# Stick breaking in a hybrid decoder trunk: the softplus rows of later key tiles summed on GpSimd for one product with the matrix of ones

## The chip, the cores and the metric

The kernel runs on one core of a Trainium2 chip. The metric is device time in microseconds of one execution; the time of a kernel is the median of its runs. Beside these runs there is one execution with the hardware profiler on, whose trace is quoted here. The core has five instruction queues that run in order and meet through semaphores: TensorE (PE, with its weight loads as PEld), VectorE (DVE), ScalarE (ACT), GpSimd (POOL) and SyncE (SP), which issues the transfers.

## The reference

Two layers of a decoder trunk on 512 tokens of width 1024, fp32. A layer normalizes its input, projects it once, and feeds five mixers: sparse attention with an index, forgetting attention, stick-breaking attention, native sparse attention and cross-attention into 256 memory tokens. Gated outputs are merged and projected back. The change is in the third mixer, which has four heads of 64:

```
z = einsum('bqhd,bshd->bhqs', q_blk, k) * scale
strict = (s_pos[None, :] < t[:, None])
log_keep = where(strict, log_sigmoid(-z), 0.0)
later = cumsum(log_keep, axis=3, reverse=True) - log_keep
a = where(strict, exp(log_sigmoid(z) + later), 0.0)
out = einsum('bhqs,bshd->bqhd', a, v)
```

For a key s, `later` is the sum of log_keep over all keys behind s and before the query. Since log_sigmoid(-z) is minus the softplus of z, and log_sigmoid(z) is z minus the softplus, the exponent is z minus the sum of the softplus over s itself and all later keys.

## The kernel before

All products that matter to precision are made of parts: an fp32 operand is split into a high part, rounded to the type fp32r that TensorE takes, and a low part, the rest; `wload` does this for every weight tile (whi on ScalarE, wlo on VectorE, line 269 and 270), and a projection (`proj`) is 24 products of 128x512.

Stick breaking is `sb_attn(pr)`, run for two pairs of heads in each layer, so for eight heads in all. Scores stand with keys in the partitions: key tile j (0 to 3, 128 keys) against the queries from 128 j on, so tile 0 is 512 columns wide, tile 1 384, tile 2 256, tile 3 128 (kept as 256, the front half zero). `begin` (line 941) makes the scores z of a tile in PSUM and then, on ScalarE and VectorE, its softplus t (`sp_t`, three buffers under the tag P). `store` (972) splits t into a high and a low row, SP[j] (the tile `sp`). `middle` (961) subtracts, by products with constant matrices added onto z, the softplus of all later keys: within the tile with a triangular matrix of -1 (`ntri`), and for each later tile with a matrix of -1 everywhere (`nones`), a product each for the high and the low row; then ScalarE takes the exponential. At the end of a pair the four tiles and two heads are multiplied with v (Yc).

Tiles are taken in the order 3, 2, 1, 0, and the `middle` of a tile stands behind the `begin` of the next. This is woven by `weave` with other work: the memory projection beside the first pair of heads, the query and index projections beside the second. A list scheduler of the framework then orders each engine's queue by its own estimates, so the places of the woven work are not fixed by the code. Its queues are in order on the chip: an instruction that waits holds up all behind it.

The pool `st` holds NST = 28 slots of 128x512 fp32 for whatever a step needs (q and k rows, squares, rotary terms); GpSimd's only work is to fill halves of K tiles with zeros (`k_stack`, line 476).

Of the kernel before, what the change touches and what calls it, by code (L numbers as in the profile page):

```python
# [10 lines left out]
F32 = mybir.dt.float32  # L11
F32R = mybir.dt.float32r
# [9 lines left out]
T = 512  # L22
KT = 8
# [2 lines left out]
EPS = 1e-6  # L26
NEG = -1e30
REPL = -3e38
NST = 28

IN_LAYOUT = (
    ('dsa_q', 256), ('dsa_ckv', 128), ('idx_q', 128), ('idx_k', 32), ('idx_w', 4), ('dsa_z', 256),
# [154 lines left out]
def trunk(ctx: ExitStack, tc: tile.TileContext, xt, memt, pos, wall, small, vec, ca, cb, out):  # L187
    nc = tc.nc
    dep_info = mybir.DependencyInfo(mybir.DependencyClass.NoSync, mybir.DependencyReason.DATA)

    def after(ins, *earlier):
        for e in earlier:
            if e is not None:
                tc.add_manual_dep(ins.ins, e.ins.name, dep_info, reason="issue order")

    def pool(name, bufs=1, **kw):
        return ctx.enter_context(tc.tile_pool(name=name, bufs=bufs, **kw))

    const = pool("const")
    big = pool("big")  # L200
    wts = pool("wts")
    st = pool("st", bufs=NST)
    wk = pool("wk")
# [4 lines left out]
    def slot(name, dt=F32, shape=(128, 512)):  # L208
        return st.tile(list(shape), dt, name=name, tag="st")

    def bank(name, tag, shape=(128, 512)):
        return ps.tile(list(shape), F32, name=name, tag=tag, bufs={"pj": 3, "S": 2, "T": 3}[tag])
# [33 lines left out]
    ntri = const.tile([128, 128], F32R, name="ntri")  # L246
    nones = const.tile([128, 128], F32R, name="nones")
# [10 lines left out]
    def mm(out_, lhsT, rhs, start, stop, **kw):  # L258
        return nc.tensor.matmul(out_, lhsT, rhs, start=start, stop=stop, **kw)  # L259
# [6 lines left out]
    def split(raw, hi, lo, scale=None):  # L266

        if scale is None:
            nc.scalar.activation(hi, raw, AF.Copy)  # L269
            nc.vector.tensor_sub(lo, raw, hi.bitcast(F32))  # L270
        else:
            nc.scalar.activation(hi, raw, AF.Copy, scale=scale)
            nc.vector.scalar_tensor_tensor(lo, raw, scale, hi.bitcast(F32), op0=OP.mult, op1=OP.subtract)
# [113 lines left out]
    def lnexp(*a, **k):  # L387
        i = nc.scalar.activation(*a, **k)
        after(i, state["set"])
        state["ln"].append(i)  # L390
        return i
# [57 lines left out]
    f32 = lambda ap: ap.bitcast(F32)  # L449
# [179 lines left out]
    def y_tiles():  # L629
        a = wk.tile([128, 2, T], F32R, name="yhi", tag="yhi", bufs=2)  # L630
        b = wk.tile([128, 2, T], F32R, name="ylo", tag="ylo", bufs=2)
        return a, b
# [52 lines left out]
    def layer(l, xs, begin):  # L685
        vo = l * V_L
        lv = SimpleNamespace(begin=begin)
# [242 lines left out]
        def sb_attn(pr):  # L930
            SPW = [512, 384, 256, 256]
            if pr == 0:
                sp = big.tile([128, 6, T], F32R, name="sp", tag="xa")
                lv.SP = [[sp[:, 2 * min(j, 2) + s, 256 * (j == 3):256 * (j == 3) + SPW[j]] for s in range(2)] for j in range(4)]
                for s in range(2):
                    nc.vector.memset(f32(lv.SP[3][s][:, 0:128]), 0.0)
            SP = lv.SP
            out = {}

            held = wk.tile([128, 1280], F32, name="sb_a", tag="sb_a", bufs=1)  # L940
            first_a = [held[:, 0:512], held[:, 512:896], held[:, 896:1152], held[:, 1152:1280]]

            def begin(e, j):

                h = 2 * pr + e
                n, w = SPW[j], T - 128 * j
                ks = slice(128 * j, 128 * j + 128)
                z = bank("sbz", "S" if j % 2 else "T")[:, :n]
                mm(z, lv.KC[h][:, ks], lv.QC[h][:, T - n:], True, False)
                mm(z, lv.KlC[h][:, ks], lv.QC[h][:, T - n:], False, False)  # L950
                mw = n - w + 128
                mm(z[:, :mw], identb, sbm[:, 256 - mw:], False, True)
                zw = z[:, n - w:]
                t = wk.tile([128, T], F32, name="sp_t", tag="P", bufs=3)[:, :w]
                nc.scalar.activation(t, zw, AF.Abs)
                lnexp(t, t, AF.Exp, scale=-1.0)
                lnexp(t, t, AF.Ln, bias=ones1)
                nc.vector.scalar_tensor_tensor(t, zw, 0.0, t, op0=OP.max, op1=OP.add)
                return e, j, z, t

            def middle(e, j, z, t):

                n = SPW[j]
                for jj in range(3, j - 1, -1):
                    for s in range(2):
                        mm(z[:, n - SPW[jj]:], ntri if jj == j else nones, SP[jj][s], False, jj == j and s == 1, skip_group_check=True)
                w = T - 128 * j
                a = first_a[j] if e == 0 else wk.tile([128, T], F32, name="sb_a", tag="PT", bufs=5)[:, :w]
                lnexp(a, z[:, n - w:], AF.Exp)
                out[e, j] = a  # L970

            def store(e, j, z, t):
                shi, slo = (x[:, SPW[j] - (T - 128 * j):] for x in SP[j])
                nc.vector.tensor_copy(shi, t)
                nc.vector.tensor_sub(slo, t, f32(shi))

            one = None
            for e in range(2):
                for j in (3, 2, 1, 0):
                    new = begin(e, j)  # L980
                    if one:
                        middle(*one)
                    store(*new)
                    one = new
                    yield
            middle(*one)

            Y = bank("Yc", "T")
            last = None
            for j in (0, 1, 2, 3):  # L990
                for e in (1, 0):
                    h = 2 * pr + e
                    m = mm(Y[64 * e:64 * e + 64, 128 * j:], lv.VC[:, j, 64 * h:64 * h + 64], out[e, j], j == 0, j == 3, skip_group_check=True)
                    after(m, last)
                    last = m
            if pr == 0:
                lv.YC = y_tiles()
            y = slot("yC")
            nc.vector.tensor_mul(y, Y, lv.ZC[0][:, pr])
            split(y, lv.YC[0][:, pr], lv.YC[1][:, pr])  # L1000
# [376 lines left out]
        if l == 0:  # L1377
            run(chain(memory_rows(), take(sp1, 1)))
            cast_constants()
            prio[0] = 3000  # L1380
            ln_phase()
            weave((sb_attn(0), 8), (chain(silu2('sb_z', lv.ZC), take(ixp, 1), take(sp1, 1), take(ixp, 1), mp), 10))
        else:
            run(take(sp1, 1))
            ln_phase()
            weave((sb_attn(0), 8), (chain(silu2('sb_z', lv.ZC), take(ixp, 1), take(sp1, 1), take(ixp, 1), mp), 10))
        tk = topk()
        nsa = nsa_proj()
        weave((sb_attn(1), 8), (chain(memq_proj(), ixp, silu2('mem_z', lv.ZE), take(nsa, 2)), 12))
        tanh_phase()  # L1390
        lv.acc = big.tile([128, KT, T], F32, name="acc", tag="xa")
# [41 lines left out]
```

## Time and profile before

| | us |
|---|---|
| median of 3 runs | 1350.59 (1350.27 to 1351.06) |
| the profiled execution | 1351.01 |
| its span, first to last instruction | 1349.2 |

The profiled execution's own time is 1.8 us longer than its span, for what lies around the first and last instruction. In the lists of instructions, a line has the source line, the engine, the operation, output<-input by the program's names, shapes and count; then busy time and the mean of one, then the idle time ahead of them on that engine with what ended it. In a timeline the first two numbers are the start and the length in microseconds; matmuls overlap, so that what one takes is read from start to start. The busiest groups are the projections' products; the weight splits on VectorE (L270) and ScalarE (L269) feed them:

```profile
L259 PE MATMUL pj<-h_hi,whi 128*128 128x512 f32 x1088 | 429.5, 396 | 0.7 <-DVE rt L433 0.7
L269 ACT ACTIVATE whi<-wraw 128x1024 fp32r<-128x1024 f32 x183 | 193.4, 1058 | 319.9 <-PE pj L259 213.9
```

### The profile page before, as it was taken

The page shows a single profiled execution, that of the slowest core. Times are in us where ns is not written, and L with a number is a line of the kernel's source. Part 1 is how long each engine was busy: PE and PEld are TensorE (multiplying, and loading weights), DVE is VectorE, ACT ScalarE, POOL GpSimd, SP SyncE. Part 2 cuts the span into 40 slices and gives each one's busy share as a digit, 9 for nine tenths or more (in the row PEclk, how much of TensorE's full clock was granted, in tenths as well). Part 3 has the DMA queues.
Part 4 walks back from the last instruction along what each step waited for, and adds up shares of the span by engine and source line. Part 5 has one row for each costly group of instructions (what it writes and reads, how often), then busy time and mean ns, then how long its engine had stood idle before and what let it go on. Part 6 is the DMA issues. An engine that isn't in the chain of part 4 may idle for free.

```text
span 1349.2 us, 18962 instructions
## 1 busy us (share of the span) xinstructions
PE 1310.1 (97%) x7240; PEld 1068.4 (79%) x7240; DVE 892.8 (66%) x1847; ACT 689.0 (51%) x1300; POOL 11.4 (1%) x28
## 2 busy tenths in 40 slices
PE   7999999999999999999999999999999999999997
PEld 6777777878888788878887777777788778887896
DVE  6887999767655444545567799995676463454554
ACT  6887834357545434434447795534574452343340
POOL 0000000000000000000000000000000000000000
PEclk9999999999999999999999999999999999999998
DMA  6442321321123132224524313222122222323231
GB/s 215 139 127 77 110 78 63 94 78 59 63 79 102 55 94 78 71 84 130 183 81 126 109 63 110 85 68 84 57 69 63 86 86 66 100 77 103 94 111 63
DMA packets 40235, 124.11 MB, mean 92 GB/s; under 512 B 4432, under 2 KB 6480, under 8 KB 40144
## 3 DMA queue, kind: packets, MB, share of 16 engines
q1 hardware_dynamic: 40144, 122.89, 28.5%
q8 instruction: 57, 0.93, 0.3%
q14 instruction: 34, 0.28, 0.1%
HBM read 118.16 MB, written 4.72 MB: 91 GB/s over the span
## 4 chain that ended last, share of the span: by engine, by line
PE 70%; ACT 6%; DVE 5%; issue 2%; DVEq 0%; ACTq 0%
PE pj L259 58%; PE Y L259 3%; PE S L259 3%; PE pt L556 3%; ACT whi L269 2%; DVE wlo L270 1%; PE hr L621 1%; ACT sw L430 1%; ACT sw L431 1%; PE sbz L259 1%; DVE P L546 0%; ACT P L547 0%; DVE score L902 0%; DVE m L901 0%; ACT Qi L848 0%
## 5 line engine op out<-in xcount | busy, mean ns | idle before, releaser
L259 PE MATMUL pj<-h_hi,whi 128*128 128x512 f32 x1088 | 429.5, 396 | 0.7 <-DVE rt L433 0.7
L259 PE MATMUL pj<-h_hi,wlo 128*128 128x512 f32 x1088 | 429.0, 394 | 0.0
L259 PE MATMUL pj<-h_lo,whi 128*128 128x512 f32 x1088 | 429.0, 394 | 0.0
L270 DVE TENSOR_TENSOR wlo<-wraw,whi 128x1024 fp32r<-128x1024 f32 x183 | 223.7, 1223 | 228.1 <-ACT whi L269 217.0
L269 ACT ACTIVATE whi<-wraw 128x1024 fp32r<-128x1024 f32 x183 | 193.4, 1058 | 319.9 <-PE pj L259 213.9
L259 PEld LDWEIGHTS pj<-h_hi,wlo 128*128 128x128 f32 x1088 | 204.5, 188 | 42.8 <-DVE wlo L270 2.3
L259 PEld LDWEIGHTS pj<-h_hi,whi 128*128 128x128 f32 x1088 | 204.6, 188 | 40.5 <-issue 1.7
L259 PEld LDWEIGHTS pj<-h_lo,whi 128*128 128x128 f32 x1088 | 204.6, 188 | 40.4 <-issue 1.8
L547 ACT ACTIVATE P<-P,nm 128x128 f32<-128x128 f32 (+3 forms) x128 | 71.6, 559 | 67.7 <-DVE nm L546 64.2
L259 PE MATMUL pj<-yhi,whi 128*128 128x512 f32 (+1 forms) x192 | 71.9, 374 | 2.9 <-ACT yhi L269 2.9
L259 PE MATMUL pj<-yhi,wlo 128*128 128x512 f32 (+1 forms) x192 | 71.6, 373 | 0.0
L259 PE MATMUL pj<-ylo,whi 128*128 128x512 f32 (+1 forms) x192 | 71.5, 372 | 0.0
L556 PE MATMUL pt<-CA,P 128*128 128x128 f32 x384 | 62.7, 277 | 2.6 <-ACT P L1274 1.3
L546 DVE CUSTOM_DVE_ANT_0 P<-S,CA 128x128 f32<-128x128 f32 (+3 forms) x104 | 47.6, 468 | 18.1 <-PE S L259 18.0
L556 PEld LDWEIGHTS pt<-CA,P 128*128 128x128 f32 x384 | 44.9, 141 | 18.2 <-ACT P L1274 6.0
L259 PE MATMUL S<-Ks,Qs 128*128 128x256 f32 (+2 forms) x160 | 51.0, 358 | 6.6 <-DVE nm L546 6.5
L394 ACT ACTIVATE G<-pj 128x512 f32<-128x512 f32 x92 | 53.6, 582 | 0.3
L902 DVE MATCH_REPLACE8 score<-m,score 128x256 f32<-128x256 f32 (+2 forms) x96 | 51.7, 541 | 0.0
L901 DVE MAX8 m<-score 128x8 f32<-128x256 f32 (+2 forms) x96 | 49.7, 546 | 0.0
L799 DVE SCALAR_TENSOR_TENSOR G<-G,pj 128x512 f32<-128x512 f32 x64 | 43.6, 681 | 3.6 <-PE pj L259 3.3
L800 DVE TENSOR_TENSOR acc<-acc,G 128x512 f32<-128x512 f32 x64 | 44.0, 688 | 0.9
L259 PEld LDWEIGHTS pj<-yhi,whi 128*128 128x128 f32 x192 | 36.2, 188 | 10.4 <-ACT yhi L269 4.0
(478 smaller groups left out, 2006.1 us busy)
## 6 DMA issues: line engine op xcount, KB each, us to landing
wraw<-in_wall_dram SPq DMA_DIRECT2D x192, 512.0 KB, 3.7
wc<-in_wall_dram SPq DMA_DIRECT2D x16, 256.0 KB, 6.1
x<-in_xt_dram SPq DMA_DIRECT2D x8, 256.0 KB, 7.0
mraw<-in_memt_dram SPq DMA_DIRECT2D x4, 512.0 KB, 4.7
xo<-in_xt_dram SPq DMA_DIRECT2D x8, 256.0 KB, 4.3
xspill<-xn SPq DMA_DIRECT2D x8, 256.0 KB, 2.2
xo<-xspill SPq DMA_DIRECT2D x8, 256.0 KB, 4.0
out_dram<-o SPq DMA_DIRECT2D x8, 256.0 KB, 2.2
```

The source lines that it names most:

```text
L259: return nc.tensor.matmul(out_, lhsT, rhs, start=start, stop=stop, **kw)
L269: nc.scalar.activation(hi, raw, AF.Copy)
L270: nc.vector.tensor_sub(lo, raw, hi.bitcast(F32))
L394: i = nc.scalar.activation(*a, **k)
L430: nc.scalar.activation(sw[a], p[b], AF.Copy)
L546: nc.vector.tensor_tensor_reduce(P, S, mask, -1.0, 3e38, OP.add, OP.min, nm)
L547: nc.scalar.activation(P, P, AF.Exp, bias=nm, scale=-1.0, accum_out=sums)
L556: nc.tensor.transpose(pt[:, 128 * j:128 * j + 128], x[:, c:c + 128], ident)
L799: nc.vector.scalar_tensor_tensor(G, G, gc, p, op0=gop, op1=OP.mult)
L800: nc.vector.tensor_add(acc, acc, G)
L901: nc.vector.max(m8, lv.work[i])
L902: nc.vector.match_replace(lv.work[i], m8, lv.work[i], REPL)
```

## The change

`middle` no longer takes the later tiles one by one. GpSimd keeps a running sum of the softplus rows of the tiles done so far (`sb_c`, two buffers: the tile's first 128 columns are copied, the others are added to the sum before), and `split_sum` splits that sum, also on GpSimd, into a high and a low row, `lv.later`, in two rows that are added to the tile `sp`. One pair of products with `nones` then stands for all later tiles. For tile 2 there is only one later tile, and its own split rows are used as before. The rows of `lv.later` are used twice by a head: the sum of tiles 3 and 2 for tile 1, then the sum of 3, 2 and 1 for tile 0, which is split only when tile 1's products have read the first. `sb_c` takes 3 KB of a partition, and the pool `st` goes from 28 slots to 26 (2 KB each).

```diff
-NST = 28
+NST = 26
...
-                sp = big.tile([128, 6, T], F32R, name="sp", tag="xa")
+                sp = big.tile([128, KT, T], F32R, name="sp", tag="xa")
...
+                lv.later = [sp[:, 6], sp[:, 7]]
...
             def middle(e, j, z, t):
 
                 n = SPW[j]
-                for jj in range(3, j - 1, -1):
-                    for s in range(2):
-                        mm(z[:, n - SPW[jj]:], ntri if jj == j else nones, SP[jj][s], False, jj == j and s == 1, skip_group_check=True)
+                for s in range(2):
+                    if j < 3:
+                        w1 = SPW[j + 1]
+                        mm(z[:, n - w1:], nones, SP[3][s] if j == 2 else lv.later[s][:, 0:w1], False, False, skip_group_check=True)
+                for s in range(2):
+                    mm(z, ntri, SP[j][s], False, s == 1, skip_group_check=True)
...
+            def split_sum():
+                c = run_["sum"]
+                hi, lo = (x[:, 0:c.shape[1]] for x in lv.later)
+                nc.gpsimd.tensor_copy(hi, c)
+                nc.gpsimd.tensor_sub(lo, c, f32(hi))
...
             def store(e, j, z, t):
...
+                w = T - 128 * j
+                if j == 3:
+                    run_["sum"] = t
+                elif j:
+
+                    c = wk.tile([128, 384], F32, name="sb_c", tag="sb_c", bufs=2)[:, :w]
+                    nc.gpsimd.tensor_copy(c[:, 0:128], t[:, 0:128])
+                    nc.gpsimd.tensor_add(c[:, 128:], t[:, 128:], run_["sum"])
+                    run_["sum"] = c
+                    if j == 2:
+                        split_sum()
...
                     if one:
                         middle(*one)
+                        if one[1] == 1:
+                            split_sum()
```

What this does to the queues, at three places. GpSimd in layer 0's first head, after the change (before, it had no row between its zero fills; `sp_t` are softplus tiles, `sb_c` sums, `sp` the split rows; 128, 256 and 384 columns belong to tiles 3 or block copies, 2 and 1):

```order
L476 MEMSET Ks_743 64x512 [waits DVE_49]
L993 COPY sb_c_649<-sp_t_639 128x128 [waits DVE_49,Pool_49]
L994 ISA
L994 TENSOR_TENSOR sb_c_649<-sp_t_639,sp_t_555 128x128
L993 COPY sb_c_707<-sp_t_695 128x128 [waits DVE_49]
L980 CAST sp_547<-sb_c_649 128x256 [waits DMAHW4_49,DMAHW2_49,DMAHW5_49,DMAHW1_49,DMAHW7_49,DMAHW0_49,Pool_49]
L994 TENSOR_TENSOR sb_c_707<-sp_t_695,sb_c_649 128x256
L981 TENSOR_TENSOR sp_547<-sb_c_649,sp_547 128x256 [waits Pool_49]
L476 MEMSET Ks_744 64x512 [waits DMAHW7_49,DMAHW4_49,Activation_49]
L980 CAST sp_547<-sb_c_707 128x384 [waits PE_49,Pool_49]
L981 TENSOR_TENSOR sp_547<-sb_c_707,sp_547 128x384 [waits PE_49,Pool_49]
```

The eight operations of a head stand in a row, with a row that prints as ISA ahead of the program's first addition, and a zero fill for a later pair of heads between.

ScalarE at the same place, where the fourth softplus (tile 0) begins; before:

```order
L477 ACTIVATE Ks_733<-pj_708 64x512 [waits PE_49]
L388 ACTIVATE sb_a_550<-sbz_635 128x256 [waits PE_49]
L478 ACTIVATE Ks_733<-pj_708 64x512
L955 ACTIVATE sp_t_749<-sbz_745 128x512 [waits PE_49]
L388 ACTIVATE sb_a_550<-sbz_686 128x384 [waits PE_49]
```

and after:

```order
L477 ACTIVATE Ks_741<-pj_716 64x512 [waits PE_49]
L388 ACTIVATE sb_a_550<-sbz_635 128x256 [waits PE_49]
L478 ACTIVATE Ks_741<-pj_716 64x512
L269 ACTIVATE yhi_847<-mraw_863 128x256 [waits DVE_49] x3
L957 ACTIVATE sp_t_757<-sbz_753 128x512 [waits PE_49,Pool_49]
L269 ACTIVATE whi_879<-wraw_877 128x1024 [waits DMAHW1_49]
```

The first step of that softplus now waits for GpSimd too, since its buffer is the one of tile 3, which GpSimd's addition reads.

TensorE in layer 0's fourth head, at the products for tile 0 (`sbz` is z; `S` and `pj` are woven work), before:

```order
L259 MATMUL pj_1637<-h_lo_385,whi_1633 128x512
L259 MATMUL sbz_1553<-sp_547,nones_105 128x256 [waits DVE_49]
L259 MATMUL sbz_1553<-sp_547,nones_105 128x256 x3
L259 MATMUL sbz_1553<-sp_547,nones_105 128x384 x2
L259 MATMUL sbz_1553<-sp_547,ntri_104 128x512 [waits DVE_49]
```

and after, with the products for tile 1 ahead of them:

```order
L259 MATMUL pj_1533<-h_hi_384,wlo_1530 128x512
L259 MATMUL sbz_1449<-sp_547,nones_105 128x256 [waits Pool_49] x2
L259 MATMUL sbz_1449<-sp_547,ntri_104 128x384 [waits DVE_49] x2
L259 MATMUL S_1617<-KE_908,Qs_1145 128x256 [waits Activation_49]
L259 MATMUL sbz_1573<-sp_547,nones_105 128x384 [waits DVE_49,Pool_49]
L259 MATMUL S_1617<-KlE_909,Qs_1145 128x256
L259 MATMUL pj_1653<-h_hi_384,whi_1649 128x512
L259 MATMUL sbz_1573<-sp_547,nones_105 128x384 [waits Pool_49]
L259 MATMUL sbz_1573<-sp_547,ntri_104 128x512 [waits DVE_49]
```

Six products have become two, each with a wait for GpSimd, and tile 1's stand closer ahead than they did.

More of the change, by code (lines that the diff above doesn't have):

```diff
@@ L936, in sb_attn @@
                     nc.vector.memset(f32(lv.SP[3][s][:, 0:128]), 0.0)
+                lv.later = [sp[:, 6], sp[:, 7]]
             SP = lv.SP
+            run_ = {}
             out = {}
```

## The prediction

> **What bounds the kernel now.** I read the page first, then the busy time of the engines in the stretches that hold the stick breaking, then the rows of its tiles, then the timeline around them. From the page, the engine shares and the chain that ended last:
>
> ```profile
> PE 1310.1 (97%) x7240; PEld 1068.4 (79%) x7240; DVE 892.8 (66%) x1847; ACT 689.0 (51%) x1300; POOL 11.4 (1%) x28
> PE 70%; ACT 6%; DVE 5%; issue 2%; DVEq 0%; ACTq 0%
> ```
>
> TensorE is the bound; GpSimd (POOL) does next to nothing. That is an average, so here are the stretches in which the stick breaking runs (the first two in layer 0, the rest in layer 1):
>
> ```profile
> core 0: us, PE busy (x) PEld busy (x) DVE busy (x) ACT busy (x) POOL busy (x), PEclk, DMA share, GB/s
> 60.00:100.00 40.00, 38.85 (x241) 31.62 (x243) 35.81 (x79) 33.99 (x74) 0.00 (x0) 1.00 0.37 121
> 100.00:138.00 38.00, 37.64 (x175) 28.84 (x172) 29.46 (x47) 27.72 (x51) 0.00 (x0) 1.00 0.24 75
> 706.00:740.00 34.00, 32.96 (x159) 25.76 (x158) 25.45 (x50) 26.52 (x52) 0.00 (x0) 1.00 0.39 124
> 740.00:775.00 35.00, 33.98 (x208) 27.59 (x207) 25.12 (x42) 23.11 (x46) 0.00 (x0) 1.00 0.33 102
> 775.00:815.00 40.00, 39.40 (x193) 29.77 (x192) 38.42 (x73) 37.04 (x69) 0.00 (x0) 1.00 0.18 57
> sum 187.00, PE 182.83 PEld 143.58 DVE 154.27 ACT 148.38 POOL 0.00; mean PE 36.57 PEld 28.72 DVE 30.85 ACT 29.68 POOL 0.00
> ```
>
> TensorE is busy in 182.8 of 187 us, at the full granted clock (1.00). So a product taken out here is time taken out, as long as TensorE, whose queue is in order, does not stand waiting instead. VectorE has 32.7 us to spare, 17%.
>
> **What is removed.** Groups of the products with the matrix of ones, by shape:
>
> ```profile
> L259 PE MATMUL sbz<-sp,nones 128*128 128x256 f32 x80 | 15.1, 300 | 1.6 <-DVE sp_t L958 1.4
> L259 PE MATMUL sbz<-sp,nones 128*128 128x384 f32 x16 | 4.1, 338 | 0.0
> ```
>
> Before, a head has 10 of 128x256 (2 for tile 2, 4 each for tiles 1 and 0) and 2 of 128x384; after, 4 and 2. Eight heads: 48 of 128x256 go. The 300 ns of a row is a pipelined length; what one costs is the step from start to start. From TensorE's timeline, first and last of a run of 128x256, first and last of a run of 128x512, and a run of six with what follows it:
>
> ```profile
> 85.24 0.28 PE L259 MATMUL pj<-yhi,whi 128*128 128x256 f32 x1
> ...
> 87.03 0.28 PE L259 MATMUL pj<-whi,yhi 128*128 128x256 f32 x1
> ...
> 133.41 1.09 PE L259 MATMUL sbz<-sp,nones 128*128 128x256 f32 x6
> 134.34 0.39 PE L259 MATMUL pj<-h_lo,whi 128*128 128x512 f32 x1
> ...
> 1084.75 0.39 PE L259 MATMUL pj<-h_lo,whi 128*128 128x512 f32 x1
> ...
> 1087.02 0.39 PE L259 MATMUL pj<-h_hi,wlo 128*128 128x512 f32 x1
> ```
>
> 15 steps in 1.79 us: 0.12 us for 256 columns. 10 steps in 2.27 us: 0.227 us for 512, so 0.17 for 384. The six (four of 256, two of 384: 1792 columns) take 0.93 us, or 0.133 per 256. I take 0.12: **48 x 0.12 = -5.8 us**, up to -6.4.
>
> **What is added.** GpSimd gets 64 instructions, 8 for a head: copy 128, add 128, split 256 (cast, subtract), copy 128, add 256, split 384. The trace shows GpSimd only filling with zeros, and VectorE doing the subtraction:
>
> ```profile
> 48.18 0.52 POOL L476 MEMSET Ks<- 64x512 f32 x1 [0.80 <-DVE Qs L458]
> 57.14 1.39 POOL L476 MEMSET KlE<- 64x256 f32 x4 [8.44 <-ACT sq L336]
> ...
> 755.76 0.56 DVE L958 SCALAR_TENSOR_TENSOR sp_t<-sbz,sp_t 128x384 f32<-128x384 f32 x1
> 756.36 0.36 DVE L974 CAST sp<-sp_t 128x384 fp32r<-128x384 f32 x1
> 756.75 0.56 DVE L975 TENSOR_TENSOR sp<-sp_t,sp 128x384 fp32r<-128x384 f32 x1
> ...
> 756.38 0.73 PE L259 MATMUL sbz<-sp,nones 128*128 128x256 f32 x4 [0.34 <-DVE sp_t L958]
> ```
>
> A fill takes 0.52 us for 512 columns and 0.35 for 256: 0.18 us plus 0.66 ns a column, one pass (the write). Lower bound of every added instruction: that line. What I take, an estimate, lets each operand read be one more pass: 0.35/0.52/0.69 us for one input of 128/256/384 columns, 0.43/0.69/0.94 for two. Upper bound: twice that, 1.9 us for the subtraction of 384, over three times VectorE's 0.56. A head is then 4.7 us of GpSimd, 37 in all; GpSimd is idle there, so the work itself costs nothing. What costs is who waits for it. The handoff from VectorE to TensorE is 0.05 us (softplus ends at 756.32, product starts at 756.38).
>
> The sum for tile 1 is made from its softplus, and split into the rows that the product for tile 2's and 3's sum has just read; tile 0's product needs the result. Before, that product needed no such step. Four of the eight heads have room: the order shows over 25 products between the two (layer 0's first head; its third has over 50). In the other four the two stand close:
>
> Second head of a pair: the softplus of tile 1 frees TensorE (0.05), which does two products of 256 (0.24), then, in layer 0, two of 384, four of 512 and one of 384 (1.42) and comes to the second tile 0 product after 1.71 us; in layer 1 (five of 512) after 1.94. GpSimd, from the same softplus: copy 0.35, add 0.69, cast 0.69, subtract 0.94, four handoffs 0.2 = 2.87. TensorE waits 1.15 and 0.95: 2.1 us.
>
> Fourth head (the order is shown above): from tile 1's second product to tile 0's second, two of 384, two of 256, one of 384, one of 512 = 0.98 us; GpSimd 0.69 + 0.94 + 0.1 = 1.73. TensorE waits 0.75, in both layers: 1.5 us.
>
> **Waits at the four places: +3.6 us** (0 at the fill's price; 12.7 at twice mine). Queued behind a waiting product are the projection's own; ScalarE and VectorE feed them from two weight tiles ahead, so they lose nothing further.
>
> **The moved order.** In layer 0's second head tile 1's scores now stand only 19 products of 512 (4.3 us) ahead of the product that needs their softplus. ScalarE's row there, by durations from the same work:
>
> ```profile
> 88.95 1.04 ACT L269 ACTIVATE whi<-wraw 128x1024 fp32r<-128x1024 f32 x1
> 90.02 0.38 ACT L477 ACTIVATE KE<-pj 64x256 fp32r<-64x256 f32 x1
> ...
> 753.56 0.49 ACT L955 ACTIVATE sp_t<-sbz 128x384 f32<-128x384 f32 x1
> 753.95 0.38 ACT L388 ACTIVATE sb_a<-sbz 128x256 f32<-128x256 f32 x1
> 754.21 0.53 ACT L388 ACTIVATE sp_t<-sp_t 128x384 f32<-128x384 f32 x1
> 754.63 0.60 ACT L955 ACTIVATE sp_t<-sbz 128x512 f32<-128x512 f32 x1
> 755.11 0.62 ACT L388 ACTIVATE sp_t<-sp_t,ones 128x384 f32<-128x384 f32 x1
> ```
>
> 1.04 + 2 x 0.38 + 0.49 + 0.38 + 0.53 + 0.60 + 0.62, and 0.56 on VectorE: 5.0, so 0.7 us of waiting, where before it was 0.2 to 0.3 (756.38 above waited 0.34). **+0.5 us**; any other moved row is as likely a gain as a loss, and I leave it at nothing.
>
> **What I cost at nothing.** Two slots fewer: outside the two stages TensorE's order changes by single rows, and the zero fills that now come later (K tiles of the second pair of heads) are read only by the next pair; the cover is that pair's distance, and if a slot is late, the projection that fills it is. GpSimd's first two-operand instruction has one ahead of it that prints as ISA and that the build adds; its length R is in no row. Its cover:
>
> ```profile
> 66.57 0.42 DVE L958 SCALAR_TENSOR_TENSOR sp_t<-sbz,sp_t 128x256 f32<-128x256 f32 x1
> ...
> 71.45 1.26 DVE L1230 SCALAR_TENSOR_TENSOR mraw<-mraw,VEC,rmem 128x256 f32<-128x256 f32 x3
> ...
> 76.91 0.50 PE L259 MATMUL sbz<-Qs,Ks 128*128 128x256 f32 x2
> ```
>
> The softplus of tile 2 is there at 66.99. Copy, R, add: 67.8 + R. The fourth softplus takes the first one's buffer (three buffers), so ScalarE waits for that add; it gets there after mraw's last row, about 73.1. TensorE needs the split sum at about 76.7 (76.91 less 0.9 for what moved behind it, plus 0.7 for rows between); it is there at 70.0 + R. So R up to 5.3 us is free, and at 6.7 TensorE waits.
>
> **Sum:** -5.8 + 3.6 + 0.5 = -1.7 us on the profiled execution's 1351.0, so 1349.3; the median of the runs is 1350.59, 0.4 below it, so **1348.9**.
>
> **Rivals.**
>
> *All covered.* GpSimd's operations near the fill's price: no wait remains, -5.8: 1344.8. For it: 187 us with an idle engine. Against: a cast and a subtraction of 384 columns take 0.96 us with handoffs even at the fill's price, and only 0.98 us lie between at two of the places.
>
> *The ISA row is long (slower).* One place, layer 0's first head. Every microsecond of R over about 6 is paid by TensorE. The nearest rows are transfers, since a row that fetches must move bytes:
>
> ```profile
> wc<-in_wall_dram SPq DMA_DIRECT2D x16, 256.0 KB, 6.1
> ```
>
> At 6.1 it is free; at twice that it costs 6.1, so -1.7 + 6.1 = +4.4: 1355.0. The Trainium skill, GPSIMD Engine Reference, section 2.1 (Instruction dispatch), says that the first call into a freshly loaded library pays about 6 us for loading it; by that the term stays near nothing. No trace here shows it.
>
> *GpSimd and VectorE shut each other out (slower).* As a mechanism here: a GpSimd instruction that reads meets a VectorE instruction with two operands in SBUF and waits it out, or the other way.
>
> ```profile
> L270 DVE TENSOR_TENSOR wlo<-wraw,whi 128x1024 fp32r<-128x1024 f32 x183 | 223.7, 1223 | 228.1 <-ACT whi L269 217.0
> ```
>
> Half of such a row is 0.6 us; two GpSimd instructions at each of the four places: 4.9 us more. And if half of GpSimd's 37 us falls on VectorE, its 32.7 us to spare go to 14, and TensorE's 4.2 us of idleness there may double. -1.7 + 4.9 + 4.2 = +7.4: 1358.0. It decides from two collisions a head on. The Trainium skill, SBUF — State Buffer, section "Who interferes with whom", states it as a lock: such a pair is exclusive for the whole instruction, and the later one fully blocks. The fills of before read nothing, so no row here bears it out or speaks against it.
>
> *The change doesn't do what it says:* the products removed lay beside another limit. TensorE's 98% in the table speaks against it; its result is within the forecast's case.
>
> **Chances.** Forecast (waits give back most; its own range 1347 to 1352) 0.37; all covered 0.30; ISA row 0.13; shut out 0.20. A measurement of this kernel tells about 0.2% (2.7 us) from no change, so faster 0.30, same 0.37, slower 0.33. Range: down to the removed products at 0.133 us each (-6.4), 1344; up to waits at twice my price (-5.8 + 12.7 + 0.5 = +7.4), which is also the lock's price, 1358.
>
> **What would show it.** TensorE's products with ones: 32 of 256 and 16 of 384. GpSimd's durations against 0.94 for the subtraction of 384. TensorE's waits for GpSimd, by place: four, each under 1.2 us. Wrong: a wait of several us near 76 (the ISA row), VectorE's wlo rows longer than 1.22 us in the two stages (the lock), or TensorE idle there over 4.2 + 3.6 + 0.5 us.

## The result, and the profile after

The changed kernel takes **1365.65 us** (median of 4 runs, 1361.85 to 1366.58) against 1350.43 for the kernel before on the same chip: a ratio of 1.0110, with a 95% interval of 1.0088 to 1.0132. It is 15.2 us slower. Forecast was 1348.9, with a range of 1344 to 1358.

The execution with the profiler on is the quickest of the four: 1361.85 us, with a span of 1360.0 against 1349.2 before. From its page, the engine shares:

```profile
PE 1310.8 (96%) x7192; PEld 1066.1 (78%) x7192; DVE 904.2 (66%) x1847; ACT 689.6 (51%) x1300; POOL 58.1 (4%) x92
```

TensorE has the 48 products fewer, and yet is busy as long as before. Its span less its busy time, the idle time, went from 39.1 to 49.2 us. VectorE has the same 1847 instructions and is busy 11.4 us longer. GpSimd has 64 instructions and 47 us more.

Where the idle time is, by ten microseconds at the end of the first stick breaking (the columns are those of the table in the prediction). Before:

```profile
100.00:110.00 10.00, 10.00 (x49) 8.16 (x46) 4.03 (x6) 2.77 (x4) 0.00 (x0) 1.00 0.39 113
...
120.00:130.00 10.00, 9.80 (x45) 7.26 (x44) 9.54 (x15) 9.83 (x17) 0.00 (x0) 1.00 0.18 55
130.00:140.00 10.00, 9.99 (x48) 7.63 (x48) 9.87 (x19) 9.24 (x22) 0.00 (x0) 1.00 0.20 58
140.00:150.00 10.00, 9.73 (x52) 7.88 (x51) 9.48 (x24) 9.70 (x19) 0.00 (x0) 1.00 0.29 102
```

After:

```profile
120.00:130.00 10.00, 8.57 (x37) 6.18 (x37) 9.68 (x13) 9.13 (x16) 3.58 (x3) 1.00 0.19 55
130.00:140.00 10.00, 8.57 (x39) 6.18 (x38) 9.87 (x18) 9.48 (x22) 0.00 (x0) 1.00 0.14 52
140.00:150.00 10.00, 8.34 (x39) 6.56 (x39) 10.00 (x24) 8.79 (x18) 4.88 (x8) 1.00 0.19 53
```

In these 30 us TensorE was busy 29.5 us before and is busy 25.5 after, while VectorE is at 97 to 100%. The rows of before say something that the prediction's table, with stretches of 34 to 40 us, had hidden: VectorE and ScalarE were at 92 to 99% here already. VectorE's spare time lies at 100 to 110, where the stick breaking has nothing for it to do.

What ended TensorE's idle time, from the list of waits (us in total, times, longest); only the rows that the stick breaking or the two slots bear on. Before:

```profile
PE sbz L259 <- DVE sp_t L958: 1.4, 3, 0.9
...
PE fox_e L259 <- ACT sel L888: 0.9, 3, 0.4
...
PE sbz L259 <- DVE sp L975: 0.7, 1, 0.7
```

After:

```profile
PE fox_e L259 <- ACT sel L888: 3.8, 4, 2.8
PE sbz L259 <- DVE sp L985: 3.0, 2, 1.5
...
PE S L259 <- DVE Qi L849: 2.6, 6, 0.9
...
PE sbz L259 <- DVE sp_t L960: 2.2, 4, 1.1
PE sbz L259 <- POOL sp L981: 2.2, 4, 0.7
...
PE sbz L259 <- DVE sp L986: 0.9, 3, 0.3
...
PE sbz L259 <- POOL sp L980: 0.6, 2, 0.4
```

The waits for GpSimd's split rows are there, 2.8 us in all, none longer than 0.7. The waits for VectorE (its rows sp, Qi and sp_t) are 8.7, where before they were 2.1. The row of `fox_e` stands outside the stick breaking, in the forgetting attention.

GpSimd's subtractions by shape (behind the count: busy time in us, mean ns, then the idle time before them):

```profile
L981 POOL TENSOR_TENSOR sp<-sb_c,sp 128x384 fp32r<-128x384 f32 x8 | 11.1, 1393 | 0.6
L981 POOL TENSOR_TENSOR sp<-sb_c,sp 128x256 fp32r<-128x256 f32 x8 | 8.8, 1096 | 0.6
```

The subtractions take 1.39 us (384 columns) and 1.10 (256) in the mean, against my 0.94 and 0.69; the shortest ones take 1.00 and 0.79. The row that prints as ISA costs nothing: the copy ahead of it ends at 65.30 us and the first addition starts at 65.35.

The granted clock is the surprise. One-microsecond stretches around the wait in the forgetting attention, and from TensorE's timeline the product that waited:

```profile
453.00:454.00 1.00, 0.00 (x0) 0.00 (x0) 0.87 (x2) 1.00 (x3) 0.00 (x0) 1.00 0.00 0
454.00:455.00 1.00, 0.00 (x0) 0.00 (x0) 0.00 (x0) 1.00 (x5) 0.00 (x0) 1.00 0.00 0
455.00:456.00 1.00, 0.23 (x1) 0.23 (x2) 0.00 (x0) 0.71 (x2) 0.00 (x0) 1.00 0.00 0
456.00:457.00 1.00, 1.00 (x5) 0.81 (x5) 0.23 (x1) 0.46 (x1) 0.00 (x0) 0.89 0.00 0
457.00:458.00 1.00, 1.00 (x7) 1.00 (x6) 1.00 (x3) 0.80 (x2) 0.00 (x0) 0.50 0.00 0
...
461.00:462.00 1.00, 1.00 (x10) 1.00 (x10) 0.00 (x0) 0.00 (x0) 0.00 (x0) 1.00 0.00 0
```

```profile
455.77 0.50 PE L259 MATMUL fox_e<-chi,sel 128*128 128x512 f32 x1 [2.78 <-ACT sel L888]
```

TensorE stands for 2.8 us, and then the clock that it is granted halves for 3.5 us: 6 or 7 products in a microsecond instead of 10 or 11. So this wait costs 2.8 us and 1.7 more. Two other stretches of this execution have the same, at 743 and 808 us; the execution before has none until its last 10 us. The three stretches together take 5.1 us (3 x 1.7) of the profiled execution. With them, the span adds up: busy time at full clock 4.4 us less, idle time 10.1 more, halved clock 5.1 more, together +10.8. The other three runs have a mean clock of 0.990 to 0.992 where this one has 0.994, and are 3.5 to 4.7 us longer; 0.002 to 0.004 of 1360 us is 2.7 to 5.4, so the clock is about what parts them (an estimate, since only one execution has a trace).

### The profile page after: what moved, and what is told of

It is laid out like the page before. It is cut to its first block, busy times and chain, and to the rows that moved or that the text cites. A ratio compares the mean times of both kernels' runs of the same rounds, so it can differ in the third digit from the quotient of the medians.

```text
span 1360.0 us, 18990 instructions
## 1 busy us (share of the span) xinstructions
PE 1310.8 (96%) x7192; PEld 1066.1 (78%) x7192; DVE 904.2 (66%) x1847; ACT 689.6 (51%) x1300; POOL 58.1 (4%) x92
## 4 chain that ended last, share of the span: by engine, by line
PE 71%; ACT 6%; DVE 5%; issue 2%; DMA 1%; POOL 0%; DVEq 0%; ACTq 0%; POOLq 0%
PE pj L259 59%; PE Y L259 3%; PE S L259 3%; PE pt L556 3%; ACT whi L269 2%; PE hr L621 1%; DVE wlo L270 1%; ACT sw L431 1%; ACT sw L430 1%; ACT P L547 1%; DMA mraw<-in_memt_dram 1%; ACT Ks L478 0%; PE fox_e L259 0%; PE sbz L259 0%; PE Yc L259 0%
## 5 line engine op out<-in xcount | busy, mean ns | idle before, releaser
L270 DVE TENSOR_TENSOR wlo<-wraw,whi 128x1024 fp32r<-128x1024 f32 x183 | 226.5, 1238 | 220.0 <-ACT whi L269 208.9
```

## The experiments

Three theories stood at the start: TensorE waits for GpSimd's rows; GpSimd and VectorE shut each other out; the two slots or the moved order cost what the forecast put at nothing. In the diffs, lines are against the kernel after the change unless "before" is named.

**The two slots alone** (against before):

```diff
-NST = 28
+NST = 26
```

> The kernel before with 26 slots in place of 28 and nothing else. If the two slots cost nothing (my step), 1350.6 within 1 us. If fewer slots are what the change pays for (the zero fills and rows that move are read late), most of the 15 us of loss: 1358 or more.

Measured: 1356.48 us against 1349.98, ratio 1.0050 (1.0033 to 1.0067): **+6.5 us** from an edit that I had put at nothing. TensorE's and VectorE's order in the stick breaking is as before; rows have moved only in the sparse attention of each layer, where the forgetting attention's projections are woven in. There, in layer 0, TensorE now stands ahead of one product, from its timeline, and in both layers the clock halves (five-microsecond stretches):

```profile
451.03 0.50 PE L259 MATMUL fox_e<-chi,sel 128*128 128x512 f32 x1 [2.79 <-ACT sel L888]
```

```profile
445.00:450.00 5.00, 2.74 (x11) 1.20 (x9) 3.52 (x11) 4.93 (x13) 0.00 (x0) 1.00 0.18 52
450.00:455.00 5.00, 3.97 (x20) 3.79 (x21) 1.89 (x3) 2.23 (x6) 0.00 (x0) 0.74 0.01 3
...
1110.00:1115.00 5.00, 4.02 (x14) 2.97 (x14) 2.72 (x8) 3.54 (x11) 0.00 (x0) 0.62 0.17 52
1115.00:1120.00 5.00, 5.00 (x31) 4.90 (x30) 1.49 (x2) 1.63 (x3) 0.00 (x0) 0.70 0.00 0
```

In the two places TensorE's idle time grew by 1.5 us only (5.5 to 7.0), but it stands in longer pieces, and the halved clock took 4.7. Over the whole execution the idle time is the same as before, 39.1 us. In layer 1 the longest wait of the place is 1.7 us, for a row maximum of the sparse attention on VectorE. Nor is it a slot that comes late in layer 0: ScalarE makes `sel` right behind its row before, without idle time, and half a microsecond earlier than before the edit (it starts at 450.36 us where it was 450.92). TensorE comes to the product earlier still, as the scheduler has ordered the sparse attention's products otherwise.

**The products alone**, without sums and with 28 slots:

```diff
-NST = 26
+NST = 28
...
-mm(z[:, n - w1:], nones, SP[3][s] if j == 2 else lv.later[s][:, 0:w1], False, False, ...)
+mm(z[:, n - w1:], nones, SP[j + 1][s], False, False, ...)
```

with the sums and `split_sum` taken out.

> Products with the matrix of ones as after the change (48 of 128x256 fewer), but each reads the split rows of the next tile alone, so the sum over the other later tiles is left out; no work on GpSimd, 28 slots. The saving alone: 1350.6 - 5.8 = 1344.8 if TensorE's products are what bounds (1344 to 1346). If the moved order by itself brings waits (tile 3's products of the third heads stood 1.5 us each in the profile after the change), 1348 to 1352. If the products removed lay beside another limit, 1350.6.

Measured: 1351.45 us (1349.80 to 1354.05, ten runs), ratio 1.0013 (1.0003 to 1.0023): **+1.5 us where -5.8 was forecast**. The page shows the saving and where it went:

```profile
PE 1304.9 (97%) x7192; PEld 1062.7 (79%) x7192; DVE 891.7 (66%) x1847; ACT 688.7 (51%) x1300; POOL 11.0 (1%) x28
```

TensorE's busy time fell by 5.2 us, as the step said, and its idle time rose by 4.3 (39.1 to 43.4). Two waits for a cast of the softplus on VectorE hold most of it, 3.6 us, in the fourth heads; a five-microsecond stretch of each:

```profile
135.00:140.00 5.00, 2.53 (x13) 1.58 (x12) 5.00 (x13) 4.95 (x14) 0.00 (x0) 1.00 0.34 103
...
795.00:800.00 5.00, 3.03 (x16) 2.09 (x15) 5.00 (x13) 4.93 (x15) 0.00 (x0) 1.00 0.38 105
```

VectorE and ScalarE are full while TensorE stands. The order has tile 3's first product close behind its scores there, so the moved order was one reading, the full engines another.

**The same with 26 slots:**

> As few_products (the sum over the later tiles but the next one is left out, no work on GpSimd), with 26 slots. TensorE's order in the stick breaking is that of few_products. If the slots and the moved order add up: 1351.5 + 6.5 = 1358, with the loss in the stretches 440 to 460 and 1100 to 1120. If what sums_unread_short lost beside the slots came from GpSimd's dependencies: below 1355.

Measured: 1359.07 us against 1350.63, ratio 1.0063 (1.0048 to 1.0078), +8.4. The slots' price comes again, 8.4 - 1.5 = 6.9.

**The sums made but not read:** the changed kernel with the product line of the second diff, so that no product waits for GpSimd.

> The changed kernel with all its work on GpSimd and its 26 slots, but the products read the split rows of the next tile alone, so no product waits for GpSimd and the sum over the other later tiles is left out; the order of every queue is nearly that of the changed kernel. If TensorE's waits for GpSimd's rows are the loss (the forecast's mechanism, mis-sized): back to 1345 to 1349. If GpSimd and VectorE shutting each other out is the loss (the rival): it stays at 1359 to 1366, with the cast of a softplus on VectorE still up to 1.0 us long. If it is the order: 1355 or more too, but with the cast at 0.2 to 0.4 us.

Measured: 1365.29 us, ratio 1.0113 (1.0098 to 1.0128), +15.3: as the changed kernel, +15.2. **TensorE's waits for GpSimd's rows, the forecast's price for the change, cost nothing that can be told from the 2 to 3 us of these intervals.** TensorE's idle time is 49.4 us, where the changed kernel has 49.2. In layer 1 the queues of TensorE, VectorE and ScalarE have the order of the changed kernel but for a row or two of TensorE's.

**The same, with 8 columns in each of GpSimd's instructions:**

```diff
-nc.gpsimd.tensor_add(c[:, 128:], t[:, 128:], run_["sum"])
+nc.gpsimd.tensor_add(c[:, 128:136], t[:, 128:136], run_["sum"][:, 0:8])
```

and the other three likewise.

> As the run before (sums on GpSimd that no product reads), but each of GpSimd's 64 instructions works on 8 columns only, so GpSimd reads next to nothing while queues and dependencies stay nearly the same; the sum over the other later tiles is left out. If the shutting out is the loss: 8 us or more less than the run before, 1347 to 1352. If the order is: as the run before. If waits for GpSimd are: both at 1345 to 1349.

Measured: 1358.75 us, ratio 1.0063 (1.0048 to 1.0078), +8.8: **6.5 us less** for GpSimd reading next to nothing. From layer 1 on, the queues of TensorE, VectorE and ScalarE are the same row for row in the two; in the first layer some rows stand elsewhere. So layer 1 shows the effect without the order's. From TensorE's timeline, the first scores of its stick breaking and the first product with v of its second pair of heads, unread sums, then short ones:

```profile
717.43 0.27 PE L259 MATMUL sbz<-Qs,Ks 128*128 128x256 f32 x1
...
824.10 2.37 PE L259 MATMUL Yc<-sb_a,VC 128*64 128x512 f32 x16
```

```profile
713.65 0.27 PE L259 MATMUL sbz<-Qs,Ks 128*128 128x256 f32 x1
...
817.35 2.38 PE L259 MATMUL Yc<-sb_a,VC 128*64 128x512 f32 x16
```

The same queues take 106.7 us with whole rows and 103.7 with short ones, of which the halved clock takes 1.7 and 3.2. So 3.0 us, or 4.5 at full clock, are shown with the order fixed. In layer 0, where some rows have moved, the same two products lie 4.0 us further apart (110.2 and 106.2). The engine lines of the two pages, the unread sums first, then the short ones:

```profile
PE 1313.9 (96%) x7192; PEld 1067.8 (78%) x7192; DVE 904.3 (66%) x1847; ACT 688.9 (51%) x1300; POOL 59.3 (4%) x92
```

```profile
PE 1312.8 (97%) x7192; PEld 1069.8 (79%) x7192; DVE 892.3 (66%) x1847; ACT 688.2 (51%) x1300; POOL 35.0 (3%) x92
```

The same 1847 instructions take VectorE 12.0 us longer when GpSimd reads whole rows. Which ones, from the groups by shape of the changed kernel:

```profile
L986 DVE TENSOR_TENSOR sp<-sp_t,sp 128x384 fp32r<-128x384 f32 x8 | 6.7, 840 | 0.1
...
L960 DVE SCALAR_TENSOR_TENSOR sp_t<-sbz,sp_t 128x384 f32<-128x384 f32 x8 | 4.4, 550 | 0.7 <-ACT sp_t L388 0.7
...
L985 DVE CAST sp<-sp_t 128x384 fp32r<-128x384 f32 x8 | 4.0, 501 | 0.1
```

and with the short rows:

```profile
L986 DVE TENSOR_TENSOR sp<-sp_t,sp 128x384 fp32r<-128x384 f32 x8 | 4.5, 559 | 0.1
...
L960 DVE SCALAR_TENSOR_TENSOR sp_t<-sbz,sp_t 128x384 f32<-128x384 f32 x8 | 4.4, 554 | 0.1
...
L985 DVE CAST sp<-sp_t 128x384 fp32r<-128x384 f32 x8 | 2.9, 356 | 0.1
```

Subtraction and cast of the softplus are hit (0.56 to 0.84 us, 0.36 to 0.50); the softplus itself, whose other operand lies in PSUM, is not (0.55 both). One meeting in the changed kernel's timeline, GpSimd's rows and then VectorE's:

```profile
121.06 0.71 POOL L980 CAST sp<-sb_c 128x384 fp32r<-128x384 f32 x1
121.86 1.87 POOL L981 TENSOR_TENSOR sp<-sb_c,sp 128x384 fp32r<-128x384 f32 x1
```

```profile
121.34 1.52 DVE L270 TENSOR_TENSOR wlo<-wraw,whi 128x1024 fp32r<-128x1024 f32 x1
122.89 2.10 DVE L849 TENSOR_TENSOR Qi<-rt,qhi 32x512 fp32r<-32x512 f32 x2
```

The weight's subtraction, 1.22 us elsewhere, takes 1.52; GpSimd's, which took 1.05 at 100.0 us, takes 1.87, and VectorE's next two 1.05 each, where the same rows took 0.68 to 0.70 before the change. The products of the index that read Qi then wait 0.9 us. The Trainium skill, SBUF — State Buffer, section "Who interferes with whom", gives the rule: an exclusive lock between GpSimd's reads and VectorE's second read port, with whoever issued first going through. The rows agree: a subtraction with both operands in SBUF is hit (0.56 to 0.84 us), the softplus with one of them in PSUM is not (0.55 both), and the cast is hit with a single operand (0.36 to 0.50); the page names casts among the operations that can enter a mode that uses both ports.

**The same eight operations on VectorE:**

> The changed kernel with the same eight operations a head on VectorE in place of GpSimd; nothing is left out. They are about 22 us more on VectorE by its own rows. If GpSimd's reads and VectorE's rows shutting each other out cost the 6.5 us between sums_unread and sums_unread_short: 1357 to 1360, and no cast over 0.45 us. If VectorE's load itself is what counts: 1364 or more.

Measured: 1369.99 us, ratio 1.0142 (1.0127 to 1.0157), +19.4. Nothing is shut out (casts of 0.22 to 0.42 us), but VectorE is 15 us busier than in few_products_26 and the kernel 10.9 us longer. So without the lock the work costs no less (10.9 us, where GpSimd's whole rows cost 6.5): this speaks for VectorE's time in the stage as what costs, whether it goes into rows or into waiting for GpSimd. It isn't shown apart from the order, which moves several hundred of TensorE's products here.

**A sum of two tiles only**, with 28 slots and in place: tile 1 reads the sum of tiles 3 and 2, tile 0 reads it and tile 1's own rows. Five variants:

```diff
+rows = [] if j == 3 else [SP[3]] if j == 2 else [lv.later] if j == 1 else [lv.later, SP[1]]
...
+elif j == 2:
+    nc.vector.tensor_add(t[:, 128:], t[:, 128:], run_["sum"])
+    run_["sum"] = t
+    split_sum()
```

> 28 slots, nothing on GpSimd, nothing left out: only the sum of tiles 3 and 2 is made (in place, on VectorE) and split; tile 1 reads it, and tile 0 reads it and tile 1's own rows. 32 products of 128x256 fewer than before: -3.8 us by the step of 0.12. The order leaves 4.6 us of other products between the fourth heads' first scores and the product that waits for their softplus (3.5 before, 1.0 after the change). If slots, moved order and the shutting out are the whole loss, it is faster than before: 1345 to 1348. If fewer products bring waits by themselves, as in few_products: 1350 to 1352.

> As two_tiles_vector, with the cast of the sum on ScalarE. 3.9 us of other products at the fourth heads. By the same reasons 1345 to 1348; if the wait for ScalarE's in-order queue shows, up to 2 us more.

> two_tiles_vector with one more turn of the woven work after tile 3 of every second head; nothing left out. If its 7 us come from where its woven rows happened to fall (stalls at 82, 90, 157 to 163, 742, 823), another draw of the order gives another time, anywhere from 1347 to 1360. If they come from the 24 rows more on VectorE: 1356 to 1359 again.

> two_tiles_vector with one more turn after tile 3 of every head; nothing left out. A second draw of the order: 1347 to 1360 if the order decides, 1356 to 1359 if VectorE's 24 rows do.

> The sum of tiles 3 and 2 alone as in two_tiles_vector, in place, but on GpSimd (24 instructions in place of 64), 28 slots, one more turn after a pair's first head; nothing left out. If GpSimd's reads cost in proportion, 24 of 64 are 2.4 us of the 6.5; with -3.8 for the products and the order as in before: 1349. With a stall or two of 2 us and the halved clock behind them: 1353 to 1357.

Measured, with the ratios' intervals: on VectorE 1357.71 (1.0034 to 1.0063), with the cast on ScalarE 1356.06 (1.0026 to 1.0054), with one more turn of the woven work (a second `yield`) 1364.24 (1.0089 to 1.0119), with a turn for every head 1356.66 (1.0031 to 1.0061), on GpSimd 1357.00 (1.0033 to 1.0063). All miss 1345 to 1348. The three orders on VectorE lie 7.6 us apart, so the order is worth several us by itself; but none of the five comes below +5.4, though all have 32 products fewer. No complete kernel of this study beats the kernel before.

**The products alone in another order:** few_products with a second `yield` a tile, and the turns of `weave` doubled to match.

> few_products (28 slots, no work on GpSimd, the sum over the later tiles but the next left out) with one more turn of the woven work between a tile's scores and what follows. At the fourth heads 3.2 us of other products now lie between the scores of tile 3 and the product that waits for their softplus, where few_products has 0.7 and 1.0 and stood 2.3 and 2.0 us. If the moved order is where the saving went: those two stalls go, 1346 to 1348. If fewer products shift the wait to another place whatever the order: 1350 to 1352 again.

Measured: 1351.53 us, ratio 1.0011 (1.0001 to 1.0021), the time of few_products. The two stalls at the fourth heads are gone, as meant, and two of 1.5 us stand at the ends of the pairs in their place. From the list of waits:

```profile
PE Yc L259 <- ACT sb_a L388: 3.0, 2, 1.5
```

So that place wasn't the cause. In both orders that were tried the saving uncovers a wait for the other engines, only at another place.

**Which engine holds the stage?** Six kernels that take from one engine or give to it: without the low parts (VectorE), few_products without them, without any product with ones (TensorE), the casts on ScalarE, without the logarithm (ScalarE), with a third product for each later tile (TensorE). The second and third start from few_products, the others from before.

```diff
-nc.vector.tensor_sub(slo, t, f32(shi))
...
-nc.vector.tensor_copy(shi, t)
+nc.scalar.activation(shi, t, AF.Copy)
...
-lnexp(t, t, AF.Ln, bias=ones1)
...
-for s in range(2):
+for s in (0, 1) if jj == j else (0, 0, 1):
```

> The kernel before without the 32 subtractions on VectorE that make the low rows of the softplus (16 us of VectorE's rows); the low rows stay zero and TensorE's products with them stay, so the low parts are left out. If VectorE's rows in the two stages set the end as much as TensorE's products: 1343 to 1348. If TensorE alone sets it and stalls come from where the order falls: 1349 to 1353.

> few_products (48 products fewer; the sum over the later tiles but the next left out) without the subtractions too (the low parts left out). If VectorE's rows held the saving back, it shows now: 5 us below the run before, 1338 to 1343. If stalls come with any order: within 2 us of the run before or of few_products.

> few_products with the other 48 products with the matrix of ones left out too (32 of 128x256, 16 of 128x384: another 6.5 us of TensorE), so no later tile is subtracted. If the stages are held by VectorE's and ScalarE's rows: 1350 to 1352 as few_products. If TensorE's products hold them: 1344 to 1346.

> The kernel before with the 32 casts of the softplus on ScalarE in place of VectorE (10 us off VectorE, 12 us more on ScalarE); nothing left out. If VectorE's rows hold the stages and ScalarE has room: 1344 to 1348. If ScalarE holds them as much, or TensorE alone: 1349 to 1353.

> The kernel before without the logarithm of the softplus (32 rows of ScalarE, some 17 us; the softplus is left at max(z, 0) + exp(-|z|)); VectorE's rows and TensorE's products are unchanged. If ScalarE's rows hold the two stages beside VectorE's: 1338 to 1346, at least as much as no_low gained. If VectorE's alone hold them: 1349 to 1352.

> The kernel before with a third product for every later tile (40 of 128x256 and 8 of 128x384 more, 6.2 us of TensorE; the high rows are subtracted twice). If TensorE is full in the stages and only the way down is closed, since VectorE and ScalarE are as full: 1356 to 1360. If TensorE has slack there: 1350 to 1353.

| | what is taken or given | us, and to before | ratio, 95% |
|---|---|---|---|
| no_ones | TensorE -12 | 1351.56, +1.5 | 0.9999 to 1.0022 |
| no_ln | ScalarE -15 | 1349.13, -0.2 | 0.9985 to 1.0004 |
| no_low | VectorE -13 | 1346.38, -3.7 | 0.9957 to 0.9981 |
| few_no_low | VectorE -14, TensorE -6 | 1347.67, -2.4 | 0.9972 to 0.9992 |
| more_ones | TensorE +6 | 1353.67, +4.4 | 1.0021 to 1.0048 |
| casts_scalar | VectorE -8, ScalarE +12 | 1365.80, +15.7 | 1.0099 to 1.0129 |

(VectorE's and ScalarE's amounts are from the engine lines of the pages, TensorE's from the products at 0.12 and 0.17 us.) Whichever engine was given work, the kernel got longer; whichever one was relieved, it gained little or nothing. Each of the six also moves several hundred of TensorE's products in the order, and the order alone was worth up to 7.6 us above, so the size of a single row shows little. In casts_scalar, for one, the same 7240 products keep TensorE busy 6.1 us longer than before (1316.2 against 1310.1), since its trace has four stretches at half clock.

The clearest is no_ones: 12 us of products less and no gain, the third kernel with fewer products that comes out at +1.2 to +1.5. In its profiled execution TensorE's idle time is 47.1 us (39.1 before), and two stretches at half clock, at 738 and 800 us, take 3.4 us more. A stretch of it:

```profile
135.00:140.00 5.00, 2.49 (x11) 1.65 (x11) 5.00 (x12) 4.90 (x13) 0.00 (x0) 1.00 0.35 105
```

TensorE is idle for half of it, and VectorE and ScalarE are full. few_no_low came out 1.3 us above no_low, not 5 below. The two lists of waits show a part of where the saved products went, no_low first, then few_no_low:

```profile
PE pt L556 <- ACT P L1275: 1.9, 4, 0.6
```

```profile
PE pt L556 <- ACT P L1286: 5.1, 6, 1.8
```

With VectorE relieved, TensorE waits for ScalarE: two new waits of 1.8 us stand right behind the two stick breakings (155 and 814 us), where the cross-attention's products need ScalarE's exponentials. And few_no_low has two stretches at half clock (449 and 735 us, 3.3 us together) where no_low has none until its last 10 us. That ScalarE holds the stage once VectorE is relieved is not shown, as no run took from both.

## Why the prediction was wrong

The medians make a ladder, each against its own runs of before: few_products +1.5, few_products_26 +8.4, sums_unread_short +8.8, sums_unread +15.3, the change +15.2. By the forecast's terms:

*The 48 products (-5.8).* Their number and price were right: 32 of 256 and 16 of 384 are left, and TensorE's busy time fell by 5.2 us in few_products. The sentence that failed is **"So a product taken out here is time taken out"**. It rested on a TensorE that is busy 98% of the two stages and a VectorE with "32.7 us to spare". That spare time was an average over stretches which hold an idle piece; in some 30 us of each layer's stage (120 to 150 and 780 to 810 us before the change) three engines are at 92 to 100% at once. What the runs showed in its place: the products' time came back as idle time of TensorE (+4.3 us in few_products), ended by VectorE's and ScalarE's rows. With the moved order in it (+0.5 in the forecast), this term is +1.5 instead of -5.3.

*The waits for GpSimd (+3.6).* The trace shows 2.8 us of them at the places named, but taking them all away (sums_unread) saves nothing, since TensorE then waits for VectorE's split rows instead (6.8 us of waits for `sp` on VectorE, 3.9 in the changed kernel). The mechanism was real and priced about right; as a cost of the change it was wrong.

*The two slots (nothing).* "If a slot is late, the projection that fills it is" was said, and then no place looked up. The place is the sparse attention of each layer, and no late slot was found there: the scheduler orders its rows otherwise, TensorE stands 2.8 us for ScalarE in layer 0 (at `fox_e`, the forgetting attention's gate rows) and 1.7 us for VectorE in layer 1, and the clock halves behind. The edit costs +6.5 alone and +6.9 beside the fewer products, of which the larger part is the halved clock.

*GpSimd's own work (nothing).* This step is where the rival that I gave 0.20 was right. GpSimd's 48 us and VectorE's rows do shut each other out: 11.4 us more on VectorE, and 6.5 us of the kernel's time, against the 9.1 (4.9 and 4.2) that the rival set for it; its +7.4 was the whole change. A quarter of GpSimd's 48 us fell on VectorE, not half of 37, and not as two collisions at each of four places: casts, subtractions and index rows are hit all over the stage. GpSimd's own price was nearly right where nothing meets it: the shortest rows of each shape add up to 4.5 us for a head, against my 4.7. In the mean a head takes 5.8; that the excess is GpSimd's own waiting for VectorE is likely, but not shown row by row.

*The ISA row.* Nothing, as costed. The Trainium skill's 6 us for loading a library (GPSIMD Engine Reference, section 2.1) do not show in this trace, where 0.05 us lie between the copy and the first addition.

*The clock.* Not in the forecast at all. It makes a long wait dearer than its length, and is part of several of the terms above.

Against the signs that the prediction named: the long wait near 76 us did not come. The sign for the lock did: VectorE's wlo rows in the two stages take 1.27 us in the mean in layer 0 (60 to 160 us) and 1.35 in layer 1 (700 to 830), where before they take 1.22, though over the whole kernel their mean rises by 1% only. Layer 1, before and after:

```profile
L270 DVE TENSOR_TENSOR wlo<-wraw,whi 128x1024 fp32r<-128x1024 f32 x18 | 22.0, 1223 | 7.9 <-ACT whi L269 7.6
```

```profile
L270 DVE TENSOR_TENSOR wlo<-wraw,whi 128x1024 fp32r<-128x1024 f32 x19 | 25.6, 1346 | 7.5 <-ACT whi L269 7.3
```

TensorE's idle time came out over its mark too: 11.8 us in the prediction's five stretches, against 4.2 before and the 8.3 named; in 60 to 160 and 700 to 830 us, which hold the two stages whole, it is 15.1 against 5.1.

What stays open: how much of the first rung is the order, since every edit draws a new one and the three orders of one kernel lay 7.6 us apart, though three kernels with fewer products in three orders came out alike; how the 6.5 us of GpSimd's work divide in layer 0, where the order moved as well; and which engine holds the stage when VectorE is relieved.

## What to carry to other kernels

Read the busy time of all engines in stretches short enough that each is either full or idle (here 5 to 10 us, not 40): work taken from the fullest engine was worth nothing here where two others were as full, and work given to an idle engine cost what it took from the one that it shuts out. An edit of buffers, however small, is to be followed to the places where it changes the order of the queues. And count a long wait of TensorE at its length and about 1.7 us more, as often as the clock halves behind it (here in half of the waits of 1.6 to 2.3 us).

## What the hardware showed beyond that

**The clock halves after short waits.** Over the 20 profiled executions, I took each stall of TensorE (idle time summed over gaps less than a microsecond apart, between the first and the last 15 us) and asked whether a stretch at half clock begins in it or within 3.5 us behind it: one does for 5 of 62 stalls of 0.85 to 1.2 us, 15 of 89 of 1.2 to 1.6, 18 of 35 of 1.6 to 2.3, and 14 of 18 of 2.3 and more. The clock then stays at 0.50 for 3.4 us, sometimes for 6.8. The same stall of the same kernel may have it in one execution and not in the next, by the mean clocks: few_products ran in 1349.8 to 1350.1 us at mean clocks of 0.994 to 0.997 and in 1353.1 to 1354.1 at 0.992. The Trainium skill, TensorE: Matmul & The Clock Gate, Part 1, has a free-running window of about 3.4 us, and an idle window of that length as the condition. The length of the halving agrees; here stalls of half that length are often enough, and the measurement decides.

**GpSimd's price for almost nothing.** With 8 columns, the shortest cast takes 0.18 us, the shortest subtraction 0.20 and the shortest addition 0.19: about the 0.18 that the prediction read out of the zero fills as the part that doesn't grow with the columns. In the mean the casts and subtractions take 0.40, since single rows take up to 1.6 us; with the copies (up to 2.1), the 64 instructions are 24 us of GpSimd (35.0 less 11.0).
